# A gather and scatter kernel: ScalarE's scalings of batch 0 behind its masks of batch 1, and other transfers between batch 0's gathers and scatters

## The chip, the cores and the metric

The kernel runs on one core of a Trainium2 chip. The metric is the device time of one execution in microseconds (us). A run gives several executions of a kernel, in rounds that alternate with the kernel before on the same chip. Chips differ a little: the kernel before has medians from 834.6 to 836.7 us in the runs below, so kernels are compared within a call, or by their ratio to the kernel before of the same rounds. A profile is one execution; its span is about 1.8 us shorter than the device time.

## The reference

```python
B, S, H = 8, 2048, 2560                     # scores [B, S, S], values [B, S, H], all float32
best_j = np.argmax(scores, axis=2)
gathered = values[b_idx, best_j, :].copy()
out = np.zeros_like(values)
np.add.at(out, (b_idx, best_j, slice(None)), gathered)
```

An output row j of a batch is values row j times the number of score rows that have their maximum at j. So a row is zero (no score row chose it), a plain copy (one did) or a multiple (two or more did). Bytes that have to move: 134 MB of scores read, 168 MB of output written, and the values rows read for copies and multiples.

## The kernel before

The kernel counts per batch how often each row is chosen, then moves rows by indirect transfers that GpSimd issues, each with a column of up to 128 row indices:

- a *copy* moves rows from DRAM to DRAM (16 transfers per batch, of which about 37% of the rows are real);
- a *zero* scatters a zero row (up to 7 columns; 12 in the last batch);
- a *multiple* is a gather into one of six slots on chip, a scaling by ScalarE, and a scatter (5 of each per batch).

SyncE loads score tiles (128 rows, 1 MB) into a room of 20 tiles; after two rounds seven of these become the slots and 13 remain. Batches 0 and 1 are counted the fast way: VectorE finds the maximum of a tile, ScalarE makes a mask with it, TensorE counts. Later batches need two passes of VectorE per tile, MAX8 and FIND_INDEX8. The code below is shortened.

```python
def compare(rows):                           # batches 0 and 1
    nc.vector.max(out=mx[:], in_=rows)
    nc.scalar.activation(out=less[:], in_=rows, func=Sign, bias=mx[:, 0:1], scale=-1.0, accum_out=n_less[:])
...
def value_steps(b, cnt_ps):                  # a generator: each yield is a place to interleave
    ...
    first = (NT, 6, 4)[min(b, 2)]            # NT = 16
    for t in range(first):
        copy_once(t)
    ...                                      # lists of rows to zero and to multiply; yields
    def gathers():
        for k in range(MCAP):                # MCAP = 5
            v = stage()
            gather(v, mi[:, k:k + 1])
            nc.scalar.activation(out=v, in_=v, func=Copy, scale=mc[:, k:k + 1])
            staged.append(v)
            if rest:
                copy_once(rest.pop(0))
    def zeros(columns):
        for k in columns:
            scatter(zrow[:], zi[:, k:k + 1], free_running)
            if rest:
                copy_once(rest.pop(0))
    if b == 0:
        zeros(range(nz))                     # nz = 7
        while tiles[0] < turn + NX:          # 27: the slots' last score tiles are masked
            yield
        gathers()
    else:
        gathers()
        zeros(range(ZHEAD))                  # ZHEAD = 4
    for k in range(MCAP):
        scatter(staged[k], mi[:, k:k + 1], ...)
    if b > 0:
        zeros(range(ZHEAD, nz))
    yield
...
for b in range(B):
    for _ in count_steps(b, cnt_ps):         # one step per score tile
        next(pending, None)                  # and one step of the batch before
    for _ in pending:
        pass
    pending = value_steps(b, cnt_ps)
    for _ in range((1, 4, 0)[min(b, 2)]):
        next(pending)
```

Each engine works through its own stream in this order. So with the condition at 27 tiles, batch 0's scalings stand in ScalarE's stream between the masks of tiles 26 and 27; batch 1 is tiles 16 to 31.

Of the kernel before, what the change touches and what calls it, by code (L numbers as in the profile page):

```python
# [36 lines left out]
def kernel(  # L37
# [8 lines left out]
    _, _, H = values.shape  # L46
    assert S == S2
    NT = S // P
# [4 lines left out]
    NX = NV * H // S  # L53
    NB = 13
    FAST = 2
# [5 lines left out]
    ZHEAD = 4  # L61
# [68 lines left out]
    turn = NX + NB  # L130
# [40 lines left out]
    def gather(v, idx, note=lambda ins: None):  # L171
        note(nc.gpsimd.indirect_dma_start(  # L172
            out=v, out_offset=None, in_=values_flat[:, :],
            in_offset=bass.IndirectOffsetOnAxis(ap=idx, axis=0), bounds_check=B * S - 1, oob_is_err=False))

    def scatter(v, idx, note=writes_out):
        note(nc.gpsimd.indirect_dma_start(  # L177
            out=out_flat[:, :], out_offset=bass.IndirectOffsetOnAxis(ap=idx, axis=0),
            in_=v, in_offset=None, bounds_check=B * S - 1, oob_is_err=False))

    vslot = [0]
    tiles = [0]

    def stage():
        v = room[:, vslot[0] * H:(vslot[0] + 1) * H]
        vslot[0] = (vslot[0] + 1) % NV
        return v
# [46 lines left out]
    def count_steps(b, cnt_ps):  # L234

        am, waiting = None, None
        for t in range(NT):
            x = b * NT + t
            if x in loads:
                n = loads[x]  # L240
                nc.sync.dma_start(out=room[:, place(x):place(x) + n * S],
                                  in_=scores[b, t * P:(t + n) * P, :].rearrange("(p r) s -> p (r s)", r=n))
            rows = room[:, place(x):place(x) + S]
            if b < FAST:
                found = compare(rows)
                if waiting is not None:
                    count_less(b, t - 1, *waiting, cnt_ps)
                waiting = found
            else:
                am = find_maxima(rows, t, am)  # L250
                if t % G == G - 1:
                    count_places(am, t, cnt_ps)
            tiles[0] = x + 1
            yield
        if waiting is not None:
            count_less(b, NT - 1, *waiting, cnt_ps)
# [62 lines left out]
    def value_steps(b, cnt_ps):  # L319
# [12 lines left out]
        def copy_once(t):  # L332
            free_running(scatter_rows_in_dram(
                nc, out_flat[:, :], values[b, t * P:(t + 1) * P, :], one_i[:, t:t + 1], last_row))


        first = (NT, 6, 4)[min(b, 2)]
        for t in range(first):
            copy_once(t)

# [66 lines left out]
# [4 lines that stand above are left out]
                nc.scalar.activation(out=v, in_=v, func=mybir.ActivationFunctionType.Copy, bias=0.0,  # L411
                                     scale=mc[:, k:k + 1])
# [10 lines that stand above are left out]

        nz = ZLAST if b == B - 1 else ZCAP
        if b == 0:
            zeros(range(nz))

            while tiles[0] < turn + NX:
                yield
            gathers()  # L430
        else:
            gathers()
            zeros(range(ZHEAD))
# [9 lines left out]
    with tc.manual_schedule(engines={ET.PE, ET.DVE, ET.Activation, ET.SP}):  # L443
        pending = iter(())
        for b in range(B):
            cnt_ps = psum_c.tile([P, NT], FP32)
            for _ in count_steps(b, cnt_ps):
                next(pending, None)
            for _ in pending:
                pass  # L450
            pending = value_steps(b, cnt_ps)
            for _ in range((1, 4, 0)[min(b, 2)]):
                next(pending)
        for _ in pending:
            pass
        full = fin.tile([1, 2], FP32)
        nc.vector.tensor_reduce(out=full[:, 0:1], in_=tots[0:1, 0, 0:B - 1], op=ALU.max, axis=mybir.AxisListType.X)
        nc.vector.tensor_reduce(out=full[:, 1:2], in_=tots[0:1, 1, :], op=ALU.max, axis=mybir.AxisListType.X)
        worst = fin.tile([P, 1], BF16)
        nc.vector.tensor_reduce(out=worst[:], in_=sole[:], op=ALU.max, axis=mybir.AxisListType.X)  # L460
        sole_ps = psum_f.tile([P, 1], FP32)
        nc.tensor.matmul(out=sole_ps[:], lhsT=ones[:], rhs=worst[:], start=True, stop=True)
        over = fin.tile([1, 4], FP32)
        nc.vector.tensor_single_scalar(out=over[:, 3:4], in_=sole_ps[0:1, :], scalar=-float(P), op=ALU.is_gt)
        nc.vector.tensor_single_scalar(out=over[:, 0:1], in_=full[:, 0:1], scalar=float(ZCAP * P), op=ALU.is_gt)
        nc.vector.tensor_single_scalar(out=over[:, 1:2], in_=full[:, 1:2], scalar=float(MCAP * P), op=ALU.is_gt)
        nc.vector.tensor_single_scalar(out=over[:, 2:3], in_=most[0:1, :], scalar=float(ZLAST * LE), op=ALU.is_gt)
        over_i = fin.tile([1, 1], INT32)
        nc.vector.tensor_reduce(out=over_i[:], in_=over[:], op=ALU.max, axis=mybir.AxisListType.X)
# [3 lines left out]
    with tc.If(more > 0):  # L473
# [32 lines left out]
        for b in range(FAST):  # L506
            cnt_ps = psum_c.tile([P, NT], FP32)
# [59 lines left out]
```

## Time and profile before

835.01 us, median of 3 runs (834.08 to 836.11); span of the profile 833.5 us.

| | before |
|---|---|
| moved by DMA | 347.13 MB |
| at 427 GB/s | 813 us |
| VectorE, ScalarE, GpSimd busy | 72%, 20%, 33% |
| first copy of batch 1 issued | 173.9 us |
| VectorE's first search of batch 2 | 181 us |
| score loads issued between 76 and 164 us | none |

### The profile page before, as it was taken

To read this page: it belongs to the slowest core of one execution; us is meant where nothing else is said; L and a number is where in the kernel's file an instruction comes from. 1 tells how busy PE (TensorE), PEld (TensorE's weight loads), DVE (VectorE), ACT (ScalarE), POOL (GpSimd) and SP (SyncE) were. 2 spreads that over 40 slices of the span, in tenths; PEclk is the share of its full clock that TensorE was granted. 3 is DMA by queue.
4 is the path that set the end of the run, shared out by engine and by line. 5 is a ranking of instruction groups with operands and counts; after the bars stand their busy time and mean duration, and the time that the engine had idled before them with its cause. 6 is when DMAs were issued, how large, how long until landed. Compare 5 with 4: busy or idle time off the path is not lost.

```text
span 833.5 us, 3112 instructions
## 1 busy us (share of the span) xinstructions
PE 31.8 (4%) x786; PEld 29.2 (4%) x786; DVE 600.4 (72%) x733; ACT 167.9 (20%) x107; POOL 276.2 (33%) x277
## 2 busy tenths in 40 slices
PE   0111100010000000000000000000000000000000
PEld 0111100010000000000000000000000000000000
DVE  5886610179999999999999999999999995000000
ACT  6663600822300003200004100023000320230230
POOL 0027300257301260162401424400605266356441
DMA  9999999999999999999999999999999999999996
GB/s 387 430 431 429 430 373 428 383 339 425 432 430 426 425 424 440 426 420 431 425 431 431 426 427 419 424 430 421 429 425 412 422 427 414 425 426 420 424 425 266
DMA packets 44951, 347.13 MB, mean 416 GB/s; under 512 B 18662, under 2 KB 18662, under 8 KB 18662
## 3 DMA queue, kind: packets, MB, share of 16 engines
q0 software_dynamic: 38736, 212.67, 61.8%
q1 hardware_dynamic: 6192, 134.22, 37.8%
q8 instruction: 6, 0.10, 0.0%
q14 instruction: 17, 0.14, 0.0%
HBM read 354.42 MB, written 300.15 MB: 785 GB/s over the span
## 4 chain that ended last, share of the span: by engine, by line
DVE 41%; issue 16%; DMA 15%; another core or an unknown queue 11%; POOL 10%; ACT 4%; PE 0%; POOLq 0%; SPq 0%; ACTq 0%; DVEq 0%
DVE am L196 16%; DVE mx L195 15%; DMA room<-in_values_dram,many_i 8%; POOL out_dram L33 5%; DMA out_dram<-room,many_i 4%; DVE mx L219 4%; DMA room<-in_scores_dram 4%; POOL out_dram L177 3%; ACT less L222 2%; POOL room L172 2%; DVE oh L372 1%; ACT room L411 1%; DVE oh_lo L205 1%; DVE lo L201 0%
## 5 line engine op out<-in xcount | busy, mean ns | idle before, releaser
L196 DVE FIND_INDEX8 am<-mx,room 128x8 uint32<-128x2048 f32 x96 | 219.4, 2285 | 0.0
L195 DVE MAX8 mx<-room 128x8 f32<-128x2048 f32 x96 | 218.8, 2280 | 0.0
L411 ACT ACTIVATE room<-room,many_c 128x2560 f32<-128x2560 f32 x40 | 96.6, 2428 | 590.0 <-DMA room<-in_values_dram,many_i 590.0
L33 POOL DMA_INDIRECT out_dram<-in_values_dram,ones_i x128 | 133.4, 1042 | 141.2 <-DVE m L343 103.1
L177 POOL DMA_INDIRECT out_dram<-room,many_i x40 | 39.1, 977 | 257.9 <-ACT room L411 254.4
L172 POOL DMA_INDIRECT room<-in_values_dram,many_i x40 | 42.6, 1065 | 122.3 <-DMA out_dram<-room,many_i 81.3
L219 DVE MAX8 mx<-room 128x8 f32<-128x2048 f32 x32 | 72.9, 2287 | 11.8 <-DMA room<-in_scores_dram 11.8
L222 ACT ACTIVATE less<-room,mx 128x2048 bf16<-128x2048 f32 x32 | 64.0, 2001 | 43.0 <-DVE sole L229 17.6
L177 POOL DMA_INDIRECT out_dram<-zrow,zero_i x61 | 60.0, 984 | 18.8 <-issue 18.8
L229 DVE TENSOR_SCALAR sole<-n_less 128x1 bf16<-128x1 f32 x32 | 4.8, 150 | 75.9 <-ACT less L222 75.6
L213 PE MATMUL cnt_ps<-oh_hi,oh_lo 128*128 128x16 bf16 x96 | 6.1, 174 | 417.3 <-DVE oh_hi L209 397.6
L232 PEld LDWEIGHTS <-less 128*128 128x128 bf16 x512 | 16.2, 104 | 143.3 <-ACT less L222 119.1
L213 PEld LDWEIGHTS <-oh_lo 128*128 128x128 bf16 x96 | 6.3, 105 | 417.2 <-DVE oh_lo L205 416.4
L372 DVE TENSOR_TENSOR oh<-lo,fill_f 128x2048 f16<-128x2048 uint32 x8 | 18.3, 2292 | 0.3
L232 PE MATMUL cnt_ps<-sole,less 128*128 128x1 bf16 x512 | 18.2, 165 | 0.0
L205 DVE TENSOR_TENSOR oh_lo<-lo,lane_f 128x512 bf16<-128x512 uint32 x24 | 16.6, 693 | 0.3
L196 DVE MATCH_VALUE_LOAD am<-mx,room 128x8 f32 x96 | 8.8, 92 | 3.3
L230 PE MATMUL cnt_ps<-sole,minus 128*128 128x16 bf16 x32 | 5.5, 172 | 144.1 <-DVE sole L229 131.7
L390 PE MATMUL l_ps<-put,oh 128*128 128x32 f16 x128 | 4.7, 188 | 71.5 <-DVE put L387 71.5
L390 PEld LDWEIGHTS <-oh 128*128 128x128 f16 x128 | 4.7, 104 | 72.6 <-DVE oh L372 62.3
L222 ACT ACTIVATION_READ_ACCUMULATOR less<-room,mx 128x1 f32 x32 | 6.0, 187 | 0.0
L209 DVE TENSOR_TENSOR oh_hi<-hi,lane_f 128x64 bf16<-128x64 uint32 x24 | 5.3, 220 | 0.0
(101 smaller groups left out, 80.4 us busy)
## 6 DMA issues: line engine op xcount, KB each, us to landing
room<-in_scores_dram SPq DMA_DIRECT2D x24, 4096.0 KB, 17.2
room<-in_scores_dram SPq DMA_DIRECT2D x9, 2048.0 KB, 11.9
room<-in_scores_dram SPq DMA_DIRECT2D x8, 1024.0 KB, 37.2
room<-in_scores_dram SPq DMA_DIRECT2D x2, 3072.0 KB, 14.9
out_dram<-in_values_dram,ones_i POOLq DMA_INDIRECT x128
out_dram<-zrow,zero_i POOLq DMA_INDIRECT x61
room<-in_values_dram,many_i POOLq DMA_INDIRECT x40, 32.7
out_dram<-room,many_i POOLq DMA_INDIRECT x40, 57.7
```

The costliest lines, as they stand in the source:

```text
L33: return eng.add_instruction(ins)
L172: note(nc.gpsimd.indirect_dma_start(out=v, out_offset=None, in_=values_flat[:, :], in_offset=bass.IndirectOffsetOnAxis(ap=idx, axis=0), bo ...
L177: note(nc.gpsimd.indirect_dma_start(out=out_flat[:, :], out_offset=bass.IndirectOffsetOnAxis(ap=idx, axis=0), in_=v, in_offset=None, bound ...
L195: nc.vector.max(out=mx[:], in_=rows)
L196: nc.vector.max_index(out=am[:, g, :], in_max=mx[:], in_values=rows)
L205: nc.vector.tensor_tensor(out=oh_lo[:], in0=lo[:].unsqueeze(2).to_broadcast([P, G, P]), in1=lane_f[:].unsqueeze(1).to_broadcast([P, G, P]) ...
L213: nc.tensor.matmul(out=cnt_ps[:], lhsT=oh_lo[:, k, :], rhs=oh_hi[:, k, :], start=(t == G - 1 and k == 0), stop=(t == NT - 1 and k == G - 1))
L219: nc.vector.max(out=mx[:], in_=rows)
L222: nc.scalar.activation(out=less[:], in_=rows, func=mybir.ActivationFunctionType.Sign, bias=mx[:, 0:1], scale=-1.0, accum_out=n_less[:])
L232: nc.tensor.matmul(out=cnt_ps[:, c:c + 1], lhsT=less[:, c * P:(c + 1) * P], rhs=w, start=False, stop=(t == NT - 1 and c == NT - 1))
L372: nc.vector.tensor_tensor(out=oh[:], in0=lo[:].unsqueeze(2).to_broadcast([P, NT, P]), in1=fill_f[:].unsqueeze(1).to_broadcast([P, NT, P]), ...
L411: nc.scalar.activation(out=v, in_=v, func=mybir.ActivationFunctionType.Copy, bias=0.0, scale=mc[:, k:k + 1])
```

## The change

Its intent: ScalarE shall finish batch 1's masks before it waits for batch 0's gathered rows, and GpSimd shall have other transfers to issue between these gathers and their scatters.

```diff
-        first = (NT, 6, 4)[min(b, 2)]
+        first = (NT, NT // 2, 4)[min(b, 2)]
...
         if b == 0:
-            zeros(range(nz))
-
-            while tiles[0] < turn + NX:
+            zeros(range(ZHEAD))
+
+            while tiles[0] < max(turn + NX, FAST * NT):
                 yield
             gathers()
+            yield
+            zeros(range(ZHEAD, nz))
...
+            if b == 1:
+                ahead, pending = pending, value_steps(b, cnt_ps)
+                next(pending)
+                for _ in ahead:
+                    pass
+                for _ in range(3):
+                    next(pending)
+                continue
             for _ in pending:
                 pass
             pending = value_steps(b, cnt_ps)
-            for _ in range((1, 4, 0)[min(b, 2)]):
+            if b == 0:
                 next(pending)
```

FAST * NT is 32, the number of tiles of batches 0 and 1. GpSimd's order was: 16 copies, 7 zeros, 5 gathers, 5 scatters, 6 copies of batch 1. It becomes: 16 copies, 4 zeros, 5 gathers, 8 copies of batch 1, 3 zeros, 5 scatters. The last block of the diff does this: `ahead` holds what is left of batch 0's steps, and batch 1's steps are begun (its first copies) before that rest is run.

## The prediction

> **What bounds the kernel now.** I read the page first: section 1 (engines), the DMA and GB/s rows of section 2, and section 3 (queues).
>
> ```profile
> PE 31.8 (4%) x786; PEld 29.2 (4%) x786; DVE 600.4 (72%) x733; ACT 167.9 (20%) x107; POOL 276.2 (33%) x277
> ...
> DMA  9999999999999999999999999999999999999996
> GB/s 387 430 431 429 430 373 428 383 339 425 432 430 426 425 424 440 426 420 431 425 431 431 426 427 419 424 430 421 429 425 412 422 427 414 425 426 420 424 425 266
> DMA packets 44951, 347.13 MB, mean 416 GB/s; under 512 B 18662, under 2 KB 18662, under 8 KB 18662
> q0 software_dynamic: 38736, 212.67, 61.8%
> q1 hardware_dynamic: 6192, 134.22, 37.8%
> ```
>
> No compute engine is full for the whole span, while the 16 DMA engines are full in every slice but the last. So the kernel is bound by moving 347.13 MB. At the 427 GB/s of its good stretches that is 347.13 / 0.427 = 813 us of the 833.5 us span. Only the remaining 20 us can be won, and only where DMA is idle or slow. The slices of GB/s point to the places: the first, the sixth (104 to 125 us), the eighth and ninth (146 to 188 us), the last. I then cut the span at those places with the view of windows (columns: stretch, its length, PE, PEld, DVE, ACT and POOL busy, PE clock, DMA share, GB/s):
>
> ```profile
> 55.00:105.00 50.00, 7.31 (x205) 6.64 (x205) 34.87 (x50) 22.95 (x22) 28.81 (x28) 1.00 1.00 429
> 105.00:120.00 15.00, 0.00 (x0) 0.00 (x0) 1.31 (x1) 0.00 (x0) 0.00 (x0) 1.00 1.02 361
> 120.00:145.00 25.00, 0.00 (x0) 0.00 (x0) 0.00 (x0) 0.00 (x0) 0.00 (x0) 1.00 1.01 426
> 145.00:190.00 45.00, 3.77 (x103) 3.35 (x102) 22.85 (x43) 22.30 (x15) 17.60 (x17) 1.00 0.94 365
> 190.00:640.00 450.00, 9.35 (x174) 9.07 (x174) 444.22 (x486) 48.37 (x20) 138.44 (x136) 1.00 1.01 427
> 640.00:820.00 180.00, 1.89 (x32) 1.55 (x32) 57.93 (x106) 36.22 (x15) 90.22 (x90) 1.00 1.02 423
> 820.00:833.40 13.40, 0.00 (x0) 0.00 (x0) 0.00 (x0) 0.00 (x0) 0.00 (x0) 1.00 0.47 184
> ```
>
> From 105 to 145 us every compute engine stands still, yet DMA is full; that stop costs nothing by itself. From 145 to 190 us it does cost: the DMA share falls to 0.94 and the rate to 365 GB/s. The timeline of ScalarE and the waits of SyncE's queue tell why:
>
> ```profile
> 101.81 2.00 ACT L222 ACTIVATE less<-room,mx 128x2048 bf16<-128x2048 f32 x1 [0.21 <-DVE sole L229]
> 103.72 0.19 ACT L222 ACTIVATION_READ_ACCUMULATOR less<-room,mx 128x1 f32 x1
> 146.85 2.43 ACT L411 ACTIVATE room<-room,many_c 128x2560 f32<-128x2560 f32 x1 [42.95 <-DMA room<-in_values_dram,many_i]
> ```
>
> ```profile
> SPq L241 <- ACT less L222: 140.7, 7, 78.3
> ```
>
> ScalarE works in program order. After the mask of tile 26 it stands at the first scaling of batch 0, 42.95 us, until the gathered rows land; those rows queue behind 16 copies and 7 zero scatters of batch 0. The masks of tiles 27 to 31 stand behind the scalings and run only from 160.7 to 171.9. Tile 40 uses the room of tile 27, so the next score load is issued at 164.8, after the longest wait of 78.3 us. The copies of batch 1 need its whole count and come at 173.9. So from 158 to 187 us both queues run low together: five scatters, then two score loads, then copies as fast as GpSimd issues them.
>
> **What the Trainium skill says.** (1) "DMA: Bandwidth & Descriptors", section "Issuing engines are not separate DMA queues": transfers of SyncE and GpSimd run on the same 16 engines and interleave. The trace agrees: 427 GB/s with both queues at work, 423 with only GpSimd's (640 to 820). Moving work between the queues' times therefore makes no bandwidth; only a hole filled counts. (2) "PSUM — Partial Sum Buffer", section "Engine vs sequencer instructions": ScalarE's, VectorE's and GpSimd's queues are strict FIFO; the 42.95 us above are that. (3) "HBM Reference", section "Specifications (TRN2)": about 716 GB/s per domain. A row copied from DRAM to DRAM is read and written there, so the 361 GB/s of 105 to 120, when nearly only batch 0's copies are left in the queue, mean up to 722 GB/s of HBM traffic. The trace fits this page, but does not prove it: the packets of 10,240 bytes take 472 ns at the middle of that stretch and 385 ns otherwise. (4) "Perfetto Trace Analysis", section "Optimization Strategy" (of "Identifying Performance Opportunities"): find the gaps on the most contended engine and what blocks there. Done above: it is DMA, 145 to 190.
>
> **The change part by part.** The comparison of the two instruction streams shows the same number of transfers: every engine's work stays, only order changes.
> - *ScalarE:* the masks of tiles 27 to 31 move ahead of batch 0's five scalings. Nothing is added. VectorE's maxima of 2.29 us set the pace of the masks, so they end about 5 x 2.3 us after 104, at about 117 us instead of 172.
> - *SyncE:* the loads of tiles 40 to 43 follow at about 109 and 114 us instead of 165 and 170. After that VectorE frees one slot of 1 MB per tile. It has 16 x 2 x 2.28 = 73 us of maxima and searches and some 12 us of the rest per batch (524 us from 181 to 705 for six batches, so 86), 5.4 us per tile, which asks for 196 GB/s.
> - *VectorE* starts batch 2 about 9 us after the last mask (172 to 181 before), at 126 instead of 181. All later searches and loads come 55 us earlier. VectorE is not the bound, so this itself gains nothing.
> - *GpSimd:* the first gather no longer has 7 zero scatters ahead but 4; the waits of the five gathers are on the same masks as before, so they are issued as early. Then come 8 copies of batch 1 (some 0.48 MB each by the counts: 37% of 1.31 MB) and three zero columns (about 2.5 MB by my estimate), and only then the scatters.
>
> The question is whether a hole remains. At 105 us some 2.3 MB of GpSimd's transfers have moved (about 45 GB/s since 55 us, as loads take nine tenths). Left before the last gather lands: copies 7.7 - 2.3 = 5.4, zeros 5.2, gathers 5.5 = 16 MB. From 105 to 131 there is room for 11.1 MB, 4.2 of them loads; so 9 MB are left at 131, at 427 - 196 = 230 GB/s some 40 us: the gathers land between 153 and 171. The first scatter is issued at about 156, the last at 174. Behind the gathers there wait 8 copies and three zeros, 6.3 MB or 27 us of work, so the queue isn't empty before 198. The second gather of batch 1 needs the first scatter to land (its slot), but then four scatters are still ahead of it. No hole is left from 105 to 250.
>
> *The sum.* 145 to 190 moved 45 x 365 = 16.4 MB, which at 427 takes 38.5 us: **6.5 us** won. 105 to 120 moved 5.4 MB, 12.7 us at 427: 2.3 us lost, of which I give back only **0.5**, as copies run nearly alone again between the loads at 114 and the ones from 131 on. Against it: the loads end 55 us earlier, so 55 us more run on GpSimd's queue alone, 423 for 427 GB/s: **0.5 us** lost. A further 0.5 for something small I overlooked. 6.5 + 0.5 - 0.5 - 0.5 = 6.0. The last 13.4 us (184 GB/s, some engines done before others) depend on how the rows are shared among the engines, which doesn't change. The start too. 835.0 - 6.0 = **829.0 us**, 0.7% less.
>
> **The rivals.** *A. A new wait takes the old one's place:* GpSimd is one FIFO, and the copies of batch 2 stand behind all of batch 1's scatters; with the scatters of batch 0 pushed back behind 11 transfers, the slots come free later, and GpSimd could let its queue run dry around 200 to 250 us. For it: GpSimd waits on slots often (81.3 us in 16 waits). Against it: score loads are there to fill, and the sum above has 6 MB in reserve. It would give 832 to 838. *B. Hidden anyway:* the rate at 145 to 190 is low because copies read and write HBM (packets above 470 ns there too), not for want of work; then only 0.94 to 1.01 of share, 45 x 0.07 = 3 us, is won: 832. *C. More is won:* with loads under all copies also the 2.3 us come back, and the last batch's lists, now 55 us early, smooth the end: 824 to 826. *D. VectorE's earlier end shortens the kernel by its 55 us:* no, after 705 it is idle for 128 us already and DMA stays full.
>
> **Range and chances.** Between A or B and C: 824 to 834. Faster by 2% would need 16.7 of the 20 us not spent at the good rate, which no part of this change touches: 0.02. Slower by 2% needs 17 us of new holes: 0.03.
>
> **What would show it.** Right: no stop of ScalarE before 117 us; a score load near 109; VectorE's batch 2 from about 126 to 650; DMA share of about 1.0 at 145 to 190 and at least 415 GB/s there; first scaling near 155; the same last 13 us. Wrong: a low share between 190 and 260 (A), share of 1 but still 370 GB/s (B), a longer tail, or a GpSimd-only phase clearly under 423 GB/s.

## The result and the profile after

The changed kernel takes **826.43 us** (median of 4 runs, 826.07 to 826.91), the kernel before 835.56 us (4 runs, 834.08 to 836.38). The ratio is 0.9893, 95% interval 0.9876 to 0.991. Ratios here are the mean time of one kernel's runs over that of the other's of the same rounds, so not quite the ratio of the medians. The gain is some 9 us, or 1.1%: within 2%, as forecast, and half as large again as forecast.

First the page of the changed kernel, its DMA rows:

```profile
DMA  9999999999999999999999999999999999999996
GB/s 383 427 436 428 432 415 416 439 421 426 421 425 428 429 429 432 430 429 428 429 420 419 428 428 431 438 420 418 426 427 421 423 425 422 424 422 424 424 427 260
```

The digits of the share are the same as before; the change only shows in the rates. The slices of 373, 383 and 339 GB/s are gone, and only the first and the last are left below 415. The windows, cut as before (the columns are the stretch, its length, busy time of PE, PEld, DVE, ACT and POOL, PE clock, DMA share and GB/s):

```profile
55.00:105.00 50.00, 8.48 (x239) 7.70 (x239) 39.14 (x53) 27.93 (x27) 25.90 (x25) 1.00 1.00 428
105.00:120.00 15.00, 2.58 (x69) 2.28 (x68) 10.85 (x35) 5.48 (x6) 5.89 (x5) 1.00 1.01 423
120.00:145.00 25.00, 0.25 (x4) 0.26 (x4) 24.79 (x21) 0.00 (x0) 6.51 (x7) 1.00 1.01 413
145.00:190.00 45.00, 0.51 (x8) 0.53 (x8) 44.58 (x36) 9.71 (x4) 3.86 (x4) 1.00 1.02 430
190.00:640.00 450.00, 10.50 (x194) 9.86 (x194) 441.12 (x541) 50.77 (x21) 144.49 (x144) 1.00 1.01 426
640.00:810.00 170.00, 0.00 (x0) 0.00 (x0) 0.00 (x0) 36.19 (x15) 84.05 (x86) 1.00 1.02 424
810.00:825.10 15.10, 0.00 (x0) 0.00 (x0) 0.00 (x0) 0.00 (x0) 0.00 (x0) 1.00 0.52 202
```

VectorE no longer stands still from 105 to 145, but that is not where the time came from. 145 to 190 went from 365 to 430 GB/s, the share from 0.94 to 1.02; 105 to 120 went from 361 to 423; 120 to 145 lost a little, 426 to 413. The last 15 us cost what they did: the same stretch of the kernel before reads

```profile
818.40:833.50 15.10, 0.00 (x0) 0.00 (x0) 0.00 (x0) 0.00 (x0) 0.00 (x0) 1.00 0.53 206
```

The timeline shows how ScalarE and GpSimd now stand (start, duration, what, in brackets the idle time before it and what ended it). First ScalarE's last mask and first scaling, then GpSimd's first copy of batch 1 and first scatter of batch 0, and last the same two of GpSimd in the kernel before, where the scatter came first:

```profile
108.84 2.00 ACT L222 ACTIVATE less<-room,mx 128x2048 bf16<-128x2048 f32 x1 [0.16 <-DVE mx L219]
...
166.72 2.43 ACT L411 ACTIVATE room<-room,many_c 128x2560 f32<-128x2560 f32 x1 [55.79 <-DMA room<-in_values_dram,many_i]
```

```profile
112.89 1.01 POOL L33 DMA_INDIRECT out_dram<-in_values_dram,ones_i  x1 [14.53 <-DVE m L343]
...
169.43 0.97 POOL L177 DMA_INDIRECT out_dram<-room,many_i  x1 [41.09 <-ACT room L411]
```

```profile
149.56 1.00 POOL L177 DMA_INDIRECT out_dram<-room,many_i  x1 [46.70 <-ACT room L411]
...
173.93 0.98 POOL L33 DMA_INDIRECT out_dram<-in_values_dram,ones_i  x1 [11.90 <-DVE m L343]
```

ScalarE now waits 55.8 us at its first scaling, longer than the 42.95 us before, and GpSimd waits 41.1 us for it (46.7 before). Neither wait costs anything, as nothing needed soon is stuck behind it: the masks are done at 110.9 (171.9 before) and batch 1's copies are out at 112.9 (173.9 before). The waits of SyncE's queue for masks fell from a longest of 78.3 us to 20.0:

```profile
SPq L241 <- ACT less L222: 78.3, 7, 20.0
```

### The profile page after: what moved, and what is told of

Same layout as the page of the kernel before. It is cut to its first block, busy times and chain, and to the rows that moved or that the text cites. A ratio compares the mean times of both kernels' runs of the same rounds, so it can differ in the third digit from the quotient of the medians.

```text
span 825.1 us, 3112 instructions
## 1 busy us (share of the span) xinstructions
PE 31.8 (4%) x786; PEld 29.2 (4%) x786; DVE 599.9 (73%) x733; ACT 168.2 (20%) x107; POOL 271.8 (33%) x277
## 2 busy tenths in 40 slices
DMA packets 44951, 347.13 MB, mean 421 GB/s; under 512 B 18662, under 2 KB 18662, under 8 KB 18662
## 4 chain that ended last, share of the span: by engine, by line
DMA 30%; DVE 26%; issue 21%; POOL 11%; another core or an unknown queue 6%; ACT 2%; PE 0%; POOLq 0%; SPq 0%; ACTq 0%; DVEq 0%
DMA room<-in_values_dram,many_i 23%; DVE am L196 9%; DVE mx L195 9%; POOL out_dram L33 6%; DVE mx L219 4%; DMA out_dram<-room,many_i 4%; POOL out_dram L177 4%; DMA room<-in_scores_dram 4%; ACT less L222 2%; POOL room L172 2%; DVE oh L372 1%; DVE oh_lo L205 1%; PE cnt_ps L232 0%; SPq L241 0%
## 5 line engine op out<-in xcount | busy, mean ns | idle before, releaser
L33 POOL DMA_INDIRECT out_dram<-in_values_dram,ones_i x128 | 130.8, 1022 | 106.4 <-DVE m L343 68.0
L172 POOL DMA_INDIRECT room<-in_values_dram,many_i x40 | 41.1, 1027 | 152.9 <-DMA out_dram<-room,many_i 134.9
L219 DVE MAX8 mx<-room 128x8 f32<-128x2048 f32 x32 | 72.8, 2286 | 11.7 <-DMA room<-in_scores_dram 11.7
L201 DVE TENSOR_SCALAR lo<-am 128x4 uint32<-128x4 uint32 x24 | 4.9, 203 | 0.8
```

Source lines behind the costliest of these rows:

```text
L33: return eng.add_instruction(ins)
L172: note(nc.gpsimd.indirect_dma_start(out=v, out_offset=None, in_=values_flat[:, :], in_offset=bass.IndirectOffsetOnAxis(ap=idx, axis=0), bo ...
```

## The experiments

Two theories were to be told apart. **Theory 1:** the hole of 145 to 190 us came from ScalarE's order: masks stuck behind scalings hold up the score loads and batch 1's count, so nothing is ready when batch 0's transfers run out. **Theory 2:** the hole was the want of transfers between gathers and scatters, and the copies and zeros put there fill it. Rival B of the prediction (copies that both read and write DRAM are slow by themselves) and the worth of VectorE's earlier start were tested too. Eleven runs of nine kernels, each against the kernel before, in five rounds.

| run | edit in words | median us | before in its call | ratio (95%) |
|---|---|---|---|---|
| e1 | masks first, nothing else | 827.68 | 836.69 | 0.9896 (0.9882 to 0.991) |
| e2 | changed, scalings between masks | 840.10 | 836.69 | 1.0041 (1.0027 to 1.0055) |
| e3 | changed, 7 zeros ahead | 825.65 | 836.69 | 0.9872 (0.9856 to 0.9887) |
| e5 | before, copies of batches 0, 1 from on-chip memory | 839.22 | 836.69 | 1.0033 (1.0019 to 1.0046) |
| a1 | changed kernel again | 826.50 | 834.61 | 0.9905 (0.9889 to 0.9922) |
| e3b | e3 again | 827.11 | 834.61 | 0.9909 (0.9892 to 0.9925) |
| e6 | changed, VectorE 55 us late | 825.65 | 834.61 | 0.9893 (0.9877 to 0.991) |
| e7 | changed, copies of batch 0 mixed | 825.25 | 834.61 | 0.9889 (0.9872 to 0.9905) |
| e9 | e1, VectorE 55 us late | 829.55 | 836.47 | 0.9913 (0.9895 to 0.9932) |
| e7b | e7 again | 826.68 | 836.47 | 0.9881 (0.9862 to 0.9899) |
| e10 | more copies mixed | 826.96 | 836.47 | 0.9882 (0.9864 to 0.99) |

All results were correct but e5's.

### e1: the masks first, and nothing else

```diff
 # the kernel before
-            while tiles[0] < turn + NX:
+            while tiles[0] < max(turn + NX, FAST * NT):
```

> The kernel before with one thing of the change alone: the scalings of batch 0 stand behind all masks of batch 1; GpSimd keeps the order of before (7 zeros ahead of the gathers, no copies between gathers and scatters). Theory 1 (the hole at 145 to 190 us came from masks, and so loads and batch 1's count, stuck behind the scalings): nearly the whole gain stays, because the score loads run on from about 105 us and the copies of batch 1 are ready when GpSimd has issued the scatters; 826 to 829 us. Theory 2 (the transfers put between gathers and scatters fill the hole): the time stays near 835, at best 832, and the DMA share is under 0.97 somewhere between 150 and 200 us.

Measured: 827.68 us, ratio 0.9896, the changed kernel's own 0.9893. Its windows:

```profile
105.00:120.00 15.00, 0.59 (x16) 0.58 (x16) 14.19 (x17) 0.00 (x0) 0.00 (x0) 1.00 1.01 425
120.00:145.00 25.00, 0.26 (x4) 0.27 (x4) 24.76 (x22) 0.00 (x0) 0.00 (x0) 1.00 1.01 422
145.00:190.00 45.00, 0.77 (x12) 0.79 (x12) 44.55 (x40) 3.15 (x2) 0.99 (x1) 1.00 1.02 432
```

No hole is left, although GpSimd issues nothing from 92 to 188.9 us (POOL is busy 0.99 us in the whole stretch). Its queue still holds gathers, and early score loads take the rest. One line of the change gives the whole gain within the interval. Theory 1 held.

### e2: the rest of the change without ScalarE's part

```diff
 # the changed kernel
-            while tiles[0] < max(turn + NX, FAST * NT):
+            while tiles[0] < turn + NX:
                 yield
             gathers()
+            while tiles[0] < FAST * NT:
+                yield
             yield
```

GpSimd's order is not quite that of the changed kernel: the scheduler puts the three zeros and two of the scatters ahead of batch 1's copies.

> The changed kernel with its scalings of batch 0 put back between batch 1's masks (after tile 26). By the stream comparison GpSimd then has 4 zeros, the gathers, 3 zeros, two scatters, 8 copies of batch 1, three scatters. Theory 1: the hole comes back, masks of tiles 27 to 31 end only at about 155 to 170 us, next score load not before 155; 833 to 838 us. Theory 2: with 3 zeros and 8 copies around, most of the gain stays; 827 to 830 us.

Measured: 840.1 us, slower than the kernel before by 0.4%. ScalarE's first scaling, GpSimd's first copy of batch 1, and the window:

```profile
141.29 2.43 ACT L411 ACTIVATE room<-room,many_c 128x2560 f32<-128x2560 f32 x1 [52.55 <-DMA room<-in_values_dram,many_i]
```

```profile
169.21 0.98 POOL L33 DMA_INDIRECT out_dram<-in_values_dram,ones_i  x1 [21.20 <-DVE m L343]
```

```profile
145.00:190.00 45.00, 3.76 (x103) 3.34 (x102) 27.87 (x47) 19.20 (x14) 17.38 (x16) 1.00 0.90 342
```

The hole is deeper than before (342 for 365 GB/s): GpSimd stands 21.2 us at a copy that waits for batch 1's count, with three scatters behind it whose rows ScalarE had scaled by 156 us. So the copies put between gathers and scatters hurt as long as the masks are late. Theory 2 fell as a cause of the whole gain; the time went even over the 838 us that theory 1 allowed.

### e3 and e3b: where the three zeros stand

```diff
 # the changed kernel
-            zeros(range(ZHEAD))
+            zeros(range(nz))
...
             gathers()
             yield
-            zeros(range(ZHEAD, nz))
```

> The changed kernel with all 7 zeros of batch 0 ahead of its gathers again, so only the 8 copies of batch 1 stand between gathers and scatters. Theory 1: no difference beyond 0.7 us (825.7 to 827.1), as the gathers only land some 10 us later and the queue still holds the copies. Theory 2: half of the filling is gone, 828 us or more.

> The changed kernel with all 7 zeros of batch 0 ahead of its gathers, once more, now beside the changed kernel. If the place of the three zeros matters not at all (theory 1), within 0.1% of it. If the 1 us that its first run seemed to win is real (a shorter last stretch, or no stretch with copies alone at 120 to 145 us), 0.1 to 0.2% under it.

Measured: first a ratio of 0.9872, which looked like a gain over the changed kernel, but that one was not in the call. Beside it, e3b has 827.11 us against 826.50 us. The place of the three zeros shows no gain; the first run's extra 0.2% was not confirmed.

### e5: copies that don't read DRAM

```diff
 # the kernel before; the result is wrong on purpose
         def copy_once(t):
+            if b < 2:
+                scatter(zrow[:], one_i[:, t:t + 1], free_running)
+                return
             free_running(...)
```

> The kernel before, but the copies of batches 0 and 1 write the zero row from on-chip memory in place of rows read from DRAM: the same rows written, the same bytes moved, the same order. The result is wrong on purpose. If the slow rate at 105 to 120 us (361 GB/s, packets of 472 ns) comes from DRAM being both source and target, that stretch goes to about 425 GB/s and the packets to 385 ns, worth 2.3 us there. Rival B of the prediction (the low rate of 145 to 190 is of the same kind) then also wins that stretch: total near 826 us. If the hole there is want of work, its DMA share stays under 0.96 and the total falls by 2.3 us and at most 1.5 more: 831 to 833.5 us.

Measured: the total is 839.22 us, a clear miss of both expectations. The windows tell two things apart:

```profile
105.00:120.00 15.00, 0.00 (x0) 0.00 (x0) 0.00 (x0) 0.00 (x0) 0.00 (x0) 1.00 1.01 413
...
145.00:190.00 45.00, 3.76 (x103) 3.34 (x102) 23.44 (x44) 22.28 (x15) 17.86 (x17) 1.00 0.90 354
```

From 105 to 120 the rate rose from 361 to 413 GB/s, and in the trace's records of transfers the packets of 10,240 bytes took 385 ns in place of 472. So that stretch was slow because its copies read DRAM, and not for want of work. From 145 to 190 it did not help at all: the share is 0.90 and the rate 354. So rival B is wrong for the hole. Not all of the hole is an idle DMA, though: the share went from 0.94 before to 1.02 after the change, the rate from 365 to 430, so about half of the loss lay in a lower rate of busy engines, for which no run shows the cause. Two other places add to the total: 640 to 810 us ran at 420 for 423 GB/s (170 x 3 / 427 = 1.2 us), and the stretch after 810 us moved 7.7 MB in 28.7 us, 10.7 us over what 427 GB/s needs, for 7.9 us in the kernel before. I suspect that scatters from on-chip memory share their rows among the 16 engines in another way than the leveling of the last batch reckons; a window inside the hole fits this (share 0.78 at 145 to 150, while rows of the first gathers were still awaited), but no run shows it. It stays open.

### a1 and e6: what VectorE's earlier start is worth

a1 is the changed kernel unaltered, for the others to be compared with.

> The changed kernel itself, unaltered, so that the variants of this call have it on the same chip in the same rounds: ratio to before 0.988 to 0.991.

```diff
 # e6: the changed kernel, after batch 1's lists
                 for _ in range(3):
                     next(pending)
+                for _ in range(24):
+                    idle = small.tile([P, 8], FP32, name="mx")
+                    nc.vector.max(out=idle[:], in_=zrow[:, 0:S])
                 continue
```

> The changed kernel with 24 useless maxima of 2.28 us (on the zero row) put on VectorE between batch 1's lists and batch 2's first search, 55 us in all, so that batch 2 starts at about 175 us as in the kernel before, but the masks and the copies of batch 1 are early. If early searches and loads are what fills the hole, the hole comes back: 830 us or more, DMA share under 0.97 in 145 to 190. If GpSimd's own queue suffices (my reckoning: 15 MB queued at 130 us, another 5.5 MB of scatters from about 155), it stays within 1.5 us of the changed kernel, with a full DMA share, and the earlier VectorE is worth nothing.

Measured: 825.65 us (825.54 to 825.76), a1 826.50 us (826.40 to 826.86). With 55 us of useless work on VectorE the kernel is no slower, even 0.1% faster. e6's windows:

```profile
120.00:145.00 25.00, 0.00 (x0) 0.00 (x0) 25.00 (x12) 0.00 (x0) 6.34 (x7) 1.00 1.02 420
145.00:190.00 45.00, 0.00 (x0) 0.00 (x0) 44.86 (x25) 12.03 (x5) 12.85 (x13) 1.00 1.02 426
```

The share stays full with no searches before 175 us, and the trace's records show no score load moving from 125 to 174 us: GpSimd's own queue suffices, as reckoned. With the copies and zeros in place, the earlier VectorE is worth nothing. For the 0.1% the trace offers a small piece, 420 for 413 GB/s at 120 to 145 (0.4 us).

### e9: both fillers taken away

e1 has early loads but nothing between gathers and scatters; e6 has the copies and zeros there but late loads. Neither has a hole. e9 takes both away, and leaves only the early masks, the early count and the first four early score tiles (their loads had moved by 119 us):

```diff
 # e1, after batch 1's lists
+            if b == 1:
+                for _ in range(24):
+                    idle = small.tile([P, 8], FP32, name="mx")
+                    nc.vector.max(out=idle[:], in_=zrow[:, 0:S])
```

> The kernel with only the masks moved ahead (GpSimd's order as before, so no copies of batch 1 between gathers and scatters), and besides the 24 useless maxima that make VectorE's batch 2 and its loads 55 us late. So neither of the two fillers is there: no early loads, no transfers between gathers and scatters. If one of them is needed, the hole comes back between 145 and 190 us (share under 0.97, 395 GB/s or less) and the time is 829 to 835 us. If the early count of batch 1 alone is enough, because its copies follow the last scatter at once, with scatters still queued, the share stays at 1.0 or more and the time is 825 to 828 us.

Measured: 829.55 us, ratio 0.9913, between the two expectations.

```profile
120.00:145.00 25.00, 0.00 (x0) 0.00 (x0) 25.00 (x13) 0.00 (x0) 0.00 (x0) 1.00 1.01 404
145.00:190.00 45.00, 0.25 (x4) 0.26 (x4) 44.76 (x30) 12.03 (x5) 19.19 (x20) 1.00 0.99 403
```

Against 427 GB/s the stretch of the hole loses 24 x 45 / 427 = 2.5 us; the kernel before lost 6.5 us there. (The 1.3 us lost at 120 to 145 are of another kind: the share is full, and by the trace's records the packets of copies took 454 ns in the mean at 120 to 125, much as at 105 to 120 in the kernel before.) So with the early count, which lets batch 1's copies follow the last scatter at once (issued at 171.3 and 170.0 us), a part of the hole closes without a filler (a share of 0.99 for 0.94), and either of the two fillers closes the rest.

### e7, e7b and e10: copies of batch 0 mixed with other transfers

If copies alone in the queue are slow, they should not stand alone. The changed kernel has 16 of them in a row.

```diff
 # the changed kernel; e7, and in e10 a 4 in place of the first NT // 2
-        first = (NT, NT // 2, 4)[min(b, 2)]
+        first = (NT // 2, NT // 2, 4)[min(b, 2)]
```

The remaining copies of batch 0 are then issued one by one between its zeros and gathers.

> The changed kernel with 8 instead of 16 copies of batch 0 ahead and the other 8 alternating with its four zeros and five gathers. Copies from DRAM to DRAM alone in the queue run slow (361 GB/s at 105 to 120 in the kernel before, 413 at 120 to 145 in the changed one). If mixing helps, 120 to 145 goes to 425 GB/s or more, worth 0.7 us: 0.05 to 0.15% faster than the changed kernel. If not, no difference.

> The mixed copies of batch 0 (8 ahead, 8 between zeros and gathers) once more: ratio to before 0.987 to 0.990. Serves to compare with the next one on the same chip.

> As the run before, with only 4 copies of batch 0 ahead of the zeros and 12 between zeros and gathers (three of these behind the gathers, among the last zeros). If what is left of copies alone between 105 and 120 us (413 GB/s in e7) still costs, 0.3 us less than e7; if the gain of e7 came from elsewhere, no difference.

Measured: e7 825.25 us (825.15 to 825.56) beside a1's 826.50 (826.40 to 826.86), 0.15% faster, just at the end of what was expected. The stretch at 120 to 145, first a1, then e7:

```profile
120.00:145.00 25.00, 0.26 (x4) 0.26 (x4) 24.79 (x20) 0.00 (x0) 6.31 (x7) 1.00 1.02 413
```

```profile
120.00:145.00 25.00, 0.26 (x4) 0.27 (x4) 24.76 (x22) 0.00 (x0) 1.83 (x2) 1.00 1.01 427
```

14 GB/s over 25 us are 0.8 us, as expected; from 105 to 120 e7 was slower than a1 (413 for 421 GB/s, 0.3 us). So the two stretches explain 0.5 of the 1.25 us, and that the mixing did it is not shown: e1, e3 and e3b have the 16 copies in a row and ran at 422, 423 and 421 GB/s from 120 to 145. e10 mixes more and gains no more: 826.96 us beside e7b's 826.68 us, where 0.3 us less was expected. **e7 is the best version in its call**: it beats the kernel before by 1.1 to 1.2% in both calls and the changed kernel by 0.15% in the one call that had both, which is no more than the same kernel's ratio moved between calls (e3 0.9872, e3b 0.9909).

## Why the prediction was right

829.0 us was forecast, with 824 to 834; 826.4 us was measured. The mechanism held in the steps that carry weight; one term of the sum was too small, and two small losses did not come.

- *The bound is DMA, and only holes or slow stretches can be won.* Right: the same 347.13 MB are moved, and the rate outside 105 to 190 us and the two ends stayed at 424 to 432 GB/s. The gain is where it was sought.
- *ScalarE's order makes the hole at 145 to 190.* Right, and shown by e1 (that part alone gives 0.9896) and e2 (all the rest without it gives 1.0041).
- *6.5 us from 145 to 190.* Right: (430 - 365) x 45 / 427 = 6.9 us.
- *0.5 us of the 2.3 us from 105 to 120.* **This is the mis-sized term.** (423 - 361) x 15 / 427 = 2.2 us came back there, less (426 - 413) x 25 / 427 = 0.8 us that copies took later: 1.4 us net. I let the masks end at 117 us and the first load come at 109; they ended at 110.9, and the load was issued at 104.1, as tile 26 was masked 4.5 us earlier in this profile than in the one before. So loads covered copies for longer. That start is partly chance: in the variants with the masks first, the last mask began anywhere from 98.2 us (e1) to 112.9 us (e3b). Rival C was right in this part. e5 shows what the term stands for: without reading DRAM the copies of that stretch run at 413 GB/s.
- *0.5 us lost to a longer phase of GpSimd's queue alone.* Not seen: 640 to 810 went from 423 to 424 GB/s. 190 to 640 reads 427 before and 426 after, but cut at 250 us it is 430 to 424 and 426 to 427, in sum nothing. The 0.5 us for something overlooked were not needed either. In all, 0.4 us more than forecast at 145 to 190, 0.9 us more at 105 to 145 and 1.0 us of losses that did not come bring the 6.0 us to 8.3; the spans of the two profiles differ by 8.4.
- *No hole from 105 to 250.* Right (no window of 10 us there has a share under 0.95), though not by my timetable. The first scaling came at 166.7 and not 155, the last at 190 and not soon after 171. This step failed, but not by the loads: by the trace's records they moved 12.1 MB from 105 to 166.7 us, just the 196 GB/s that I gave them. GpSimd's queue moved 14.1 MB in that time, where the reckoning has 5.4 + 5.2 + 1.1 = 11.7 MB up to the end of the first gather. So by that estimate over 2 MB issued later moved before the first gather was complete; I had reckoned as if the queue emptied strictly in order. Why it doesn't is not shown. Rival A, a new hole behind the later scatters, did not come: GpSimd waits longer for slots (134.9 us in 25 waits for 81.3 in 16), with work queued.
- *VectorE's 55 us gain nothing by themselves.* Right where GpSimd's queue is filled otherwise, shown by e6. Its batch 2 started at 120 us (126 was forecast). (A slip without effect: before the change VectorE ended at 701.5 us, not 705.)
- *The end is unchanged.* Right: 15.1 us at 202 GB/s for 15.1 us at 206.

What the prediction didn't see is how little of the change is needed. It reckoned with the copies and zeros behind the gathers as the reserve that prevents a hole; e1 has none of them and no hole either, because early loads do the same: without these (e9) a part of the hole is back.

## What to carry to other kernels

When DMA is the bound, look at the rate per stage, and where it dips ask what the empty queue is waiting for; here one in-order engine held finished tiles behind a long wait, and moving that wait behind the last work that others needed gave the whole gain. A wait that lengthens is harmless if nothing needed stands behind it, and putting more transfers between a request and its use can hurt when they depend on the late work themselves (e2). An engine that finishes earlier was worth nothing by itself under a full DMA (e6); where the queue would run low its loads filled the gap (e1 beside e9, 432 for 403 GB/s, though the intervals of the two ratios overlap).

## What the Trainium skill lacked or had wrong

- No page gives the rate of row copies from DRAM to DRAM that GpSimd issues by index. "HBM Reference", "Specifications (TRN2)", has 716 GB/s per domain; the one row on copies between HBM tensors in "DMA: Bandwidth & Descriptors" ("Latency and other measured facts") is about tiles from the other queues. Here a stretch with hardly anything else ran at 361 GB/s moved, and at 413 when the same rows were written from on-chip memory.
- "DMA: Bandwidth & Descriptors", "Queues, rings and completion order", says that an engine goes round its queues packet by packet. The trace's records of the kernel before agree: from 80 to 100 us, with both queues full, they have 267 packets of SyncE's queue and 267 of GpSimd's (191 and 190 from 65 to 80). The bytes are far from even, as the packets differ in size: 382 GB/s for loads with rows of 32 KB, 44 for GpSimd (65 to 80). What the page doesn't say is that a skipped row of an indirect transfer takes a turn too: the records have 17,974 packets of 4 bytes in GpSimd's queue, as many as skipped rows (269 transfers of 128 indices, less 20,762 rows moved: 13,670) and 16 per transfer (4,304) together. About two thirds of GpSimd's turns from 65 to 80 us went to such packets (125 of 190).
- No page has a cause for the long packets in the hole itself. From 174 to 189 us in the kernel before, most packets of 10,240 bytes took 385 ns, and 12 of 340 over 1 us, so the mean is 463 ns. In e5, where copies don't read DRAM, the mean was 503 ns at 184 to 189 us. They stay unexplained.
